# Loading the first three units of an instance norm in shares of partitions

## The chip, the cores and the metric

The kernel runs on one core of one Trainium2 chip. The metric is the device time of one execution in microseconds (us). The times of the kernel before are from three runs; the profile is from one more execution, recorded by the hardware profiler.

## The reference

```python
B, G, C_per_g, H, W = 4, 8, 16, 256, 256
mu = x.mean(axis=(3, 4), keepdims=True)
var = ((x - mu) ** 2).mean(axis=(3, 4), keepdims=True)
out = (x - mu) / np.sqrt(var + 1e-5) * gamma[None, :, :, None, None]
```

Each of the 4 x 8 x 16 = 512 images of 256 x 256 float32 numbers is normalized by its own mean and variance and scaled by the gamma of its channel. The input and the output have 134 MB each, and every number is read once and written once.

## The kernel before

The 512 images are cut into U = 32 units of 16 images. A unit is a tile of 128 partitions with 8192 numbers (32 KB) in each: S = 8 partitions hold one image. In DRAM a unit is one contiguous block of 4 MB, row after row. There are AHEAD = 6 slots in SBUF, named xt0 to xt5; unit u lives in slot u modulo 6, is normalized in place and is stored from there.

Before the loop, `load` (L48) is called for units 0 to 5. Units 1 and 3 are issued on ACT's DMA queue, and units 0, 2, 4 and 5 on SP's. In the profile SP's queue is q1 and ACT's is q10. GpSimd issues two small DMAs of its own: L54 writes a tile of zeros named touch (16 partitions of 128 numbers) into the output, where the first unit's result is written later, and L55 loads gamma. After the loads the program text has 60 no-ops on ACT. Small constants follow, the load of the table for the square root (L78) and a first small root on ACT, and a spread of gamma by 8 matrix products (L88).

The loop over the units does the following for each of them:

- L107: VectorE sums each row of the unit into the first column of st.
- L108: ACT squares the unit and accumulates the squares of each row into the second column. The squares themselves go to a tile named junk.
- L116: TensorE multiplies by a block matrix with -1/65536, which gives every partition the negated mean and mean square of its image.
- L117 to L127: VectorE and ACT make the variance, the root, its reciprocal and the scale, each of one column.
- L130: VectorE adds the negated mean and multiplies by the scale, in place.
- The store of the unit is issued on ACT's queue.
- `load` for unit u + 6 is issued on SP's queue. It goes into the slot that the store is still reading, so SP waits for that store to land.

The order of instructions on each engine is that of the program text. Each DMA on the hardware queues (SP's and ACT's) signals its completion on one of eight semaphores, which are handed out in turn. Where a semaphore is handed out again, the issuing queue first waits for the DMA that had it, unless another wait already implies that.

Of the kernel before, what the change touches and what calls it, by code (L numbers as in the profile page):

```python
# [1 line left out]

# [4 lines left out]

F32 = mybir.dt.float32
U8 = mybir.dt.uint8
ALU = mybir.AluOpType  # L10
ACTF = mybir.ActivationFunctionType
AX = mybir.AxisListType


@with_exitstack
def kernel(
    ctx: ExitStack,
    tc: tile.TileContext,
    x: bass.AP,
    gamma: bass.AP,  # L20
    out: bass.AP,
):
    nc = tc.nc
    B, G, C, H, W = x.shape
    P = nc.NUM_PARTITIONS
    HW = H * W
    n_ch = B * G * C
    S = 8
    K = P // S
    F = HW // S  # L30
    U = n_ch // K
    NG = (G * C) // K
    AHEAD = 6
    assert HW % S == 0 and (G * C) % K == 0

    xv = x.rearrange("b g c h w -> (b g c h w)").rearrange("(u p f) -> u p f", p=P, f=F)
    ov = out.rearrange("b g c h w -> (b g c h w)").rearrange("(u p f) -> u p f", p=P, f=F)
    gv = gamma.rearrange("g c -> (g c)")

    data = ctx.enter_context(tc.tile_pool(name="data", bufs=1))  # L40
    singles = ctx.enter_context(tc.tile_pool(name="singles", bufs=1))
    psum = ctx.enter_context(tc.tile_pool(name="psum", bufs=4, space=bass.MemoryType.PSUM))
    ctx.enter_context(tc.manual_schedule())

    slots = [data.tile([P, F], F32, name=f"xt{i}") for i in range(AHEAD)]

    def load(u, queue):
        queue.dma_start(out=slots[u % AHEAD][:], in_=xv[u])  # L48


    g_row = singles.tile([1, G * C], F32, name="g_row")
    touch = singles.tile([16, 128], F32, name="touch")
    nc.vector.memset(touch[:], 0.0)  # L53
    nc.gpsimd.dma_start(out=ov[0][0::S, 0:128], in_=touch[:])  # L54
    nc.gpsimd.dma_start(out=g_row[:], in_=gv[None, :])  # L55
    for u in range(AHEAD):
        load(u, nc.scalar if u in (1, 3) else nc.sync)

    for _ in range(60):
        nc.scalar.nop()  # L60

    eps_t = singles.tile([P, 1], F32, name="eps_t")
    nc.gpsimd.memset(eps_t[:], 1e-5)
    one = singles.tile([1, 1], F32, name="one")
    nc.gpsimd.memset(one[:], 1.0)
    navg = singles.tile([P, K, S], F32, name="navg")
    nc.gpsimd.memset(navg[:], -1.0 / HW)  # L67
    nc.gpsimd.affine_select(  # L68
        out=navg[:], in_=navg[:], pattern=[[-S, K], [0, S]], compare_op=ALU.is_ge,
        fill=0.0, base=0, channel_multiplier=1,  # L70
    )
    nc.gpsimd.affine_select(  # L72
        out=navg[:], in_=navg[:], pattern=[[S, K], [0, S]], compare_op=ALU.is_ge,
        fill=0.0, base=S - 1, channel_multiplier=-1,
    )
    navg_w = navg[:].rearrange("p k s -> p (k s)")
    root_eps = singles.tile([P, 1], F32, name="root_eps")
    nc.scalar.activation(out=root_eps[:], in_=eps_t[:], func=ACTF.Sqrt)  # L78
    g_rep = singles.tile([1, NG, K, S], F32, name="g_rep")
    g_ps = psum.tile([P, NG], F32, name="g_ps", bufs=1)  # L80
    g_col = singles.tile([P, NG], F32, name="g_col")

    nc.vector.tensor_copy(  # L83
        out=g_rep[:],
        in_=g_row[:].rearrange("o (n k) -> o n k", n=NG).unsqueeze(3).to_broadcast([1, NG, K, S]),
    )
    for n in range(NG):
        nc.tensor.matmul(  # L88
            out=g_ps[:, n : n + 1],
            lhsT=g_rep[:, n].rearrange("o k s -> o (k s)"),  # L90
            rhs=one[:],
            start=True, stop=True,
        )
    nc.vector.tensor_copy(out=g_col[:], in_=g_ps[:])  # L94

    junk = singles.tile([P, F], U8, name="junk")

    st = singles.tile([P, U, 2], F32, name="st")
    nvar = singles.tile([P, U], F32, name="nvar")
    std = singles.tile([P, U], F32, name="std")  # L100
    rstd = singles.tile([P, U], F32, name="rstd")
    scale = singles.tile([P, U], F32, name="scale")

    squares = []
    for u in range(U):
        t = slots[u % AHEAD]
        nc.vector.reduce_sum(out=st[:, u, 0:1], in_=t[:], axis=AX.X)  # L107
        square = nc.scalar.activation(  # L108
            out=junk[:], in_=t[:], func=ACTF.Square, accum_out=st[:, u, 1:2],
        )  # L110
        if u:

            tc.declare_no_dep(square.ins, squares[-1].ins, reason="junk, ordered by the root between")
        squares.append(square)
        ps = psum.tile([P, 2], F32, name="ps")
        nc.tensor.matmul(out=ps[:], lhsT=navg_w, rhs=st[:, u], start=True, stop=True)  # L116
        nc.vector.tensor_scalar(  # L117
            out=nvar[:, u : u + 1], in0=ps[:, 0:1], scalar1=ps[:, 0:1],
            scalar2=ps[:, 1:2], op0=ALU.mult, op1=ALU.add,
        )  # L120
        nc.scalar.activation(  # L121
            out=std[:, u : u + 1], in_=nvar[:, u : u + 1], func=ACTF.Sqrt,
            bias=eps_t[:], scale=-1.0,
        )
        nc.vector.reciprocal(out=rstd[:, u : u + 1], in_=std[:, u : u + 1])  # L125
        g = u % NG
        nc.vector.tensor_mul(  # L127
            out=scale[:, u : u + 1], in0=rstd[:, u : u + 1], in1=g_col[:, g : g + 1],
        )
        nc.vector.tensor_scalar(  # L130
            out=t[:], in0=t[:], scalar1=ps[:, 0:1], scalar2=scale[:, u : u + 1],
            op0=ALU.add, op1=ALU.mult,
        )
        nc.scalar.dma_start(out=ov[u], in_=t[:])
        if u + AHEAD < U:
            load(u + AHEAD, nc.sync)


# [1 line left out]
_INS = ['x', 'gamma']  # L140
_OUTS = [((4, 8, 16, 256, 256), 'float32')]


# [23 lines left out]
```

## Time and profile before

| What | Value |
|---|---|
| Median of three runs | 627.39 us (626.88 to 627.53) |
| Span of the profiled execution | 624.9 us |
| VectorE, ACT, TensorE busy | 443.4, 238.8, 21.4 us |
| HBM read and written | 134.22 and 134.23 MB, 430 GB/s over the span |
| Load on SP's queue, issue to landing | 38.5 us, median of 30 |
| Load on ACT's queue, issue to landing | 31.5 us, median of 2 |
| Store, issue to landing | 62.5 us, median of 32 |
| Waits of SP's queue for stores | 534.4 us in 26 waits |

The profiled execution has no time beside its span, which runs from the first to the last instruction. The median of the runs is 2.5 us longer than that span: it takes in what lies around the instructions. The landing times of loads and stores are longer than the 9.6 us in which 4 MB would move at 436 GB/s, since two queues share the 16 DMA engines and a transfer also waits for those ahead of it in its queue. In a row of the table of windows, the columns are: the window, its length, the busy time of PE, PEld, DVE, ACT and POOL with the number of instructions, the granted clock, the mean share of the DMA engines, and GB/s. In a row of the chain of waits, they are the start, the length and what the time went to.

### The profile page before, as it was taken

To read this page: it belongs to the slowest core of one execution; us is meant where nothing else is said; L and a number is where in the kernel's file an instruction comes from. 1 tells how busy PE (TensorE), PEld (TensorE's weight loads), DVE (VectorE), ACT (ScalarE), POOL (GpSimd) and SP (SyncE) were. 2 spreads that over 40 slices of the span, in tenths; PEclk is the share of its full clock that TensorE was granted. 3 is DMA by queue.
4 is the path that set the end of the run, shared out by engine and by line. 5 is a ranking of instruction groups with operands and counts; after the bars stand their busy time and mean duration, and the time that the engine had idled before them with its cause. 6 is when DMAs were issued, how large, how long until landed. Compare 5 with 4: busy or idle time off the path is not lost.

```text
span 624.9 us, 631 instructions
## 1 busy us (share of the span) xinstructions
PE 21.4 (3%) x80; PEld 19.5 (3%) x80; DVE 443.4 (71%) x163; ACT 238.8 (38%) x98; POOL 2.4 (0%) x11
## 2 busy tenths in 40 slices
PE   0200000000000000000000000000000000000000
PEld 0200000000000000000000000000000000000000
DVE  0588999999776687666786767867668676687730
ACT  0444444444443234432344423444224442244400
POOL 1000000000000000000000000000000000000000
DMA  8999999999999999999999999999999999999998
GB/s 370 436 426 430 422 434 436 436 436 437 432 424 433 436 436 424 436 436 434 436 436 432 422 436 436 434 426 436 436 434 436 436 434 419 436 436 434 426 436 369
DMA packets 9282, 268.46 MB, mean 430 GB/s; under 512 B 1072, under 2 KB 1088, under 8 KB 1088
## 3 DMA queue, kind: packets, MB, share of 16 engines
q10 hardware_dynamic: 4896, 142.61, 52.9%
q1 hardware_dynamic: 4320, 125.83, 46.8%
q0 software_dynamic: 64, 0.01, 0.0%
q14 instruction: 2, 0.02, 0.0%
HBM read 134.22 MB, written 134.23 MB: 430 GB/s over the span
## 4 chain that ended last, share of the span: by engine, by line
another core or an unknown queue 61%; DMA 17%; DVE 15%; SPq 1%; PE 1%; issue 0%; ACT 0%
DVE st L107 10%; DMA xt<-in_x_dram 10%; DMA out_dram<-xt 8%; DVE xt L130 5%; SPq L48 1%; PE ps L116 1%; ACT std L121 0%; DVE nvar L117 0%; DVE rstd L125 0%; DVE scale L127 0%
## 5 line engine op out<-in xcount | busy, mean ns | idle before, releaser
L107 DVE TENSOR_REDUCE st<-xt 128x1 f32<-128x8192 f32 x32 | 277.9, 8685 | 100.4 <-DMA xt<-in_x_dram 100.4
L108 ACT ACTIVATE junk<-xt 128x8192 uint8<-128x8192 f32 x32 | 225.0, 7030 | 275.1 <-DMA xt<-in_x_dram 231.9
L130 DVE TENSOR_SCALAR xt<-xt,ps,scale 128x8192 f32<-128x8192 f32 x32 | 145.6, 4550 | 1.2
L121 ACT ACTIVATE std<-nvar,eps_t 128x1 f32<-128x1 f32 x32 | 9.4, 294 | 79.6 <-DVE nvar L117 79.6
L116 PE MATMUL ps<-st,navg 128*128 128x2 f32 x64 | 17.9, 349 | 557.1 <-DVE st L107 557.1
L116 PEld LDWEIGHTS ps<-st,navg 128*128 128x128 f32 x64 | 16.0, 311 | 558.9 <-issue 558.9
L117 DVE TENSOR_SCALAR nvar<-ps 128x1 f32<-128x1 f32 x32 | 9.2, 287 | 23.8 <-PE ps L116 23.8
L125 DVE RECIPROCAL rstd<-std 128x1 f32<-128x1 f32 x32 | 5.2, 164 | 11.6 <-ACT std L121 11.6
L83 DVE COPY g_rep<-g_row 1x1024 f32<-1x1024 f32 x1 | 0.7, 681 | 14.3 <-DMA g_row<-in_gamma_dram 14.3
L108 ACT ACTIVATION_READ_ACCUMULATOR junk<-xt 128x1 f32 x32 | 6.0, 186 | 0.0
L127 DVE TENSOR_TENSOR scale<-rstd,g_col 128x1 f32<-128x1 f32 x32 | 5.1, 159 | 1.1
L88 PE MATMUL g_ps<-one,g_rep 1*128 1x1 f32 x16 | 3.5, 347 | 16.1 <-DVE g_rep L83 16.1
L88 PEld LDWEIGHTS g_ps<-one,g_rep 1*128 1x128 f32 x16 | 3.5, 325 | 16.1 <-issue 16.1
L94 DVE COPY g_col<-g_ps 128x8 f32<-128x8 f32 x1 | 0.2, 166 | 3.7 <-PE g_ps L88 3.7
L78 ACT ACT_TABLE_LOAD x1 | 1.3, 1283 | 1.7 <-PEq L151 1.7
L53 DVE MEMSET touch<- 16x128 f32 x1 | 0.2, 165 | 0.9 <-PEq L151 0.9
L54 POOL DMA_DIRECT2D out_dram<-touch x1 | 0.6, 619 | 0.8 <-DVE touch L53 0.8
L55 POOL DMA_DIRECT2D g_row<-in_gamma_dram x1 | 0.5, 487 | 0.0
L68 POOL TENSOR_SCALAR_AFFINE_SELECT navg<-navg 128x128 f32<-128x128 f32 x1 | 0.4, 400 | 0.1
L72 POOL TENSOR_SCALAR_AFFINE_SELECT navg<-navg 128x128 f32<-128x128 f32 x1 | 0.4, 399 | 0.1
L67 POOL MEMSET navg<- 128x128 f32 x1 | 0.2, 232 | 0.0
L78 ACT ACTIVATE root_eps<-eps_t 128x1 f32<-128x1 f32 x1 | 0.2, 203 | 0.0
(6 smaller groups left out, 0.6 us busy)
## 6 DMA issues: line engine op xcount, KB each, us to landing
out_dram<-xt ACTq DMA_DIRECT2D x32, 4096.0 KB, 62.5
xt<-in_x_dram SPq DMA_DIRECT2D x30, 4096.0 KB, 38.5
xt<-in_x_dram ACTq DMA_DIRECT2D x2, 4096.0 KB, 31.5
out_dram<-touch POOLq DMA_DIRECT2D x1, 8.0 KB, 9.1
g_row<-in_gamma_dram POOLq DMA_DIRECT2D x1, 0.5 KB, 13.3
```

The source lines that it names most:

```text
L48: queue.dma_start(out=slots[u % AHEAD][:], in_=xv[u])
L78: nc.scalar.activation(out=root_eps[:], in_=eps_t[:], func=ACTF.Sqrt)
L83: nc.vector.tensor_copy(out=g_rep[:], in_=g_row[:].rearrange("o (n k) -> o n k", n=NG).unsqueeze(3).to_broadcast([1, NG, K, S]),)
L88: nc.tensor.matmul(out=g_ps[:, n : n + 1], lhsT=g_rep[:, n].rearrange("o k s -> o (k s)"), rhs=one[:], start=True, stop=True,)
L107: nc.vector.reduce_sum(out=st[:, u, 0:1], in_=t[:], axis=AX.X)
L108: square = nc.scalar.activation(out=junk[:], in_=t[:], func=ACTF.Square, accum_out=st[:, u, 1:2],)
L116: nc.tensor.matmul(out=ps[:], lhsT=navg_w, rhs=st[:, u], start=True, stop=True)
L117: nc.vector.tensor_scalar(out=nvar[:, u : u + 1], in0=ps[:, 0:1], scalar1=ps[:, 0:1], scalar2=ps[:, 1:2], op0=ALU.mult, op1=ALU.add,)
L121: nc.scalar.activation(out=std[:, u : u + 1], in_=nvar[:, u : u + 1], func=ACTF.Sqrt, bias=eps_t[:], scale=-1.0,)
L125: nc.vector.reciprocal(out=rstd[:, u : u + 1], in_=std[:, u : u + 1])
L127: nc.vector.tensor_mul(out=scale[:, u : u + 1], in0=rstd[:, u : u + 1], in1=g_col[:, g : g + 1],)
L130: nc.vector.tensor_scalar(out=t[:], in0=t[:], scalar1=ps[:, 0:1], scalar2=scale[:, u : u + 1], op0=ALU.add, op1=ALU.mult,)
```

## The change

Units 0, 1 and 2 are no longer loaded by one DMA each. A table gives for each of them a list of shares (first partition, step), and `load` issues one DMA for each share, on the same queue as before. For units 0 and 1 these are every 8th partition from 0, every 8th from 4, every 4th from 2 and every 2nd from 1: 16, 16, 32 and 64 partitions. For unit 2 they are every 4th from 0, every 4th from 2 and every 2nd from 1: 32, 32 and 64. All other units are loaded as before. The large and small transfers on the hardware queues are 72 in all, in place of 64. The 60 no-ops are dropped from the text.

```diff
+    shares = {
+        0: ((0, S), (S // 2, S), (S // 4, S // 2), (1, 2)),
+        1: ((0, S), (S // 2, S), (S // 4, S // 2), (1, 2)),
+        2: ((0, S // 2), (S // 4, S // 2), (1, 2)),
+    }
+
     def load(u, queue):
-        queue.dma_start(out=slots[u % AHEAD][:], in_=xv[u])
+        for first, step in shares.get(u, ((0, 1),)):
+            queue.dma_start(out=slots[u % AHEAD][first::step], in_=xv[u][first::step])
...
     for u in range(AHEAD):
         load(u, nc.scalar if u in (1, 3) else nc.sync)
-
-    for _ in range(60):
-        nc.scalar.nop()
```

## The prediction

> **What bounds the kernel now.** I read the page first, for its engines, its slices and its DMA queues; then the chain of work that ended last; then a table of windows over the whole span; and last the packet records of the trace, one record for each row of 32 KB that a DMA engine moves.
>
> ```profile
> span 624.9 us, 631 instructions
> ...
> PE 21.4 (3%) x80; PEld 19.5 (3%) x80; DVE 443.4 (71%) x163; ACT 238.8 (38%) x98; POOL 2.4 (0%) x11
> ...
> DMA  8999999999999999999999999999999999999998
> ...
> q10 hardware_dynamic: 4896, 142.61, 52.9%
> q1 hardware_dynamic: 4320, 125.83, 46.8%
> ...
> L107 DVE TENSOR_REDUCE st<-xt 128x1 f32<-128x8192 f32 x32 | 277.9, 8685 | 100.4 <-DMA xt<-in_x_dram 100.4
> ```
>
> The busiest compute engine is VectorE with 71%, and it idles 100.4 us for loads. The two queues (q10 is ACT's, q1 is SP's) fill 52.9 + 46.8 = 99.7% of the time of 16 DMA engines. So the bound is the DMA engines, in every slice. From the chain of waits:
>
> ```profile
> 0.80 21.80 DMA xt<-in_x_dram
> ...
> 33.10 4.55 DVE xt L130
> ...
> 546.72 38.51 DMA xt<-in_x_dram
> ...
> 595.73 4.55 DVE xt L130
> ```
>
> Units 0 and 1 share the engines and arrive together at 22.6. The first store is issued after 33.10 + 4.55 = 37.65; until then the two rings hold loads only, and the six loads (25.2 MB at 436 GB/s, 58 us) outlast that. The last apply ends at 600.3, while stores run to 623. At 436 GB/s the store of one unit takes 9.6 us, so the last store could be issued some 13 us later without moving the end. Compute therefore has slack at both ends, and the time is: start of the first row + 512 rows for each DMA engine + what follows the last row. The windows show each of these:
>
> ```profile
> 0.00:1.50 1.50, 0.00 (x0) 0.00 (x0) 0.17 (x1) 0.00 (x0) 0.35 (x5) 1.00 0.00 0
> 1.50:2.00 0.50, 0.00 (x0) 0.00 (x0) 0.00 (x0) 0.28 (x1) 0.50 (x2) 1.00 1.98 590
> 2.00:3.00 1.00, 0.00 (x0) 0.00 (x0) 0.00 (x0) 1.00 (x1) 0.93 (x5) 1.00 0.70 229
> ...
> 4.00:22.00 18.00, 3.54 (x16) 3.48 (x16) 0.85 (x2) 0.00 (x0) 0.00 (x0) 1.00 1.00 432
> 22.00:38.00 16.00, 0.56 (x2) 0.50 (x2) 14.20 (x6) 7.42 (x3) 0.00 (x0) 1.00 1.00 434
> 38.00:44.00 6.00, 0.00 (x0) 0.00 (x0) 6.00 (x1) 5.92 (x1) 0.00 (x0) 1.00 0.92 350
> ...
> 100.00:580.00 480.00, 14.51 (x52) 13.03 (x52) 356.12 (x130) 190.63 (x78) 0.00 (x0) 1.00 1.00 433
> ```
>
> The last two numbers are the DMA share and GB/s, counted by the packets that start in the window. In 1.50:2.00, 590 GB/s are nine rows, and a share of 1.98 is 1.98 x 0.5 x 16 / 9 = 1.76 us a row. In 100:580 a row takes 32.8 KB x 16 / 433 = 1.21 us. So the first rows are stretched by about 0.5 us. In 38:44 the same happens a second time: the packet records show 10.3 us of stretch in all, 0.64 an engine, where the first store joins the loads. Nowhere else is there anything to win: between 100 and 580 the rows stand back to back. The sum for one engine: first row from 1.80 to 2.67, ending between 3.48 and 4.06 in the records; 511 more at 1.21 (619); last rows end between 622.7 and 623.6; the span ends at 624.9. The runs' median is 627.39, so 2.5 us lie around the span, and I leave them as they are.
>
> **The change, part by part.** *The no-ops:* ACT's instructions in the profile hold no no-op, and the table load starts at 1.72, right behind the two load issues (0.80 + 0.88). Dropping them removes nothing: 0.
>
> *Eight more transfers.* SP gets five more (three for unit 0, two for unit 2), ACT three. Bytes, rows and the 8 rows that each engine moves of a unit stay the same; only their order changes (rows 0, 4, 2, 6, then the odd ones of each eight). Each transfer adds one semaphore packet per engine: the records give it 9 ns, the next row beginning 6 ns after it. 8 x 6 ns = 0.05 us.
>
> *Issue time.* Two ACT issues took 0.88 us, so 0.44 each. Four shares keep SP and ACT until about 2.6, but the first is issued at 0.80 as before, and each engine then has a row from each ring, until 1.80 + 2 x 1.21 = 4.2 at least; the second shares, issued by 1.7, are there in time. Cost 0. Were a share later than its predecessor's row, an engine would idle for the difference.
>
> *New waits on the issuing queues.* There are eight completion semaphores for the hardware queues, and eight shares now take them all. In the built order ACT's issue of unit 3 waits for unit 1's first share, SP's three shares of unit 2 for unit 0's first, unit 1's second and unit 0's second share, unit 4 for unit 0's third, and unit 5 for unit 1's last. With two rings taking turns, row n of an engine ends at about 2.5 + 1.21 n. Those shares end with rows 1, 2, 3, 4, 7 and 16: at 3.7, 4.9, 6.1, 7.3, 11.0 and 21.9, and the semaphore follows some 0.5 later (unit 0 and 1: row end 22.1, landing 22.6). Needed are units 2 and 3 by 22, unit 4 by 41 (when unit 2 is done) and unit 5 by 61. The margins are 14 us and more. Behind ACT's waiting issue stand its table load (1.28 us) and the small root: they move from 1.7 to about 6 and end near 7.5, and the first square needs them at 22.62. Behind SP's waits stand only its other loads, of which the seventh waits for store 0 anyway. The first square and reduction wait for four semaphores in place of one, some tens of ns on an engine with slack. Cost 0 in all; a margin used up would cost idle DMA time one for one.
>
> *The ramp.* No hardware transfer of 16 rows is in the trace, so its start has to be bounded. If the first rows began and ran no better, the gain is 0. If all began at 1.80 and took 1.21, they would end at 3.01 in place of 3.74 on the engine that ends last (4.06 at worst): at most 0.7 to 1.0 us. In the other direction, each of the three boundaries that both rings now reach together could stretch a row as the first ones are stretched: 3 x 0.6 = 1.8 us more. The nearest rows speak for little: the first rows end together (3.48 to 4.06) however early they began, and the row that began last, at 2.67, took only 1.22. So what they wait for was common to all, and a shorter list of descriptors for each engine need not shorten it. At the boundary between units 0, 1 and units 2, 3 near 22 us, both rings end a transfer, and the windows on its two sides show 432 and 434 GB/s with no gap in the records. I take 0.25 us of gain here, a third of the smaller bound.
>
> [...]
>
> The sum: 0 + 0.05 + 0 + 0 - 0.25 = -0.2 us, so a span of 624.7 and 627.39 - 0.2 = **627.2 us**.
>
> **The rivals.** *Drain at each boundary (slower).* The engine finishes a share, signals, and starts the next only when the writes are confirmed. What a transfer takes beyond its data bounds the price: 21.8 us from issue to landing less 8.39 MB at 436 GB/s (19.2) is 2.6. The three boundaries common to both rings would give 7.8 us, and 635.0; at the 0.6 of a stretched first row, 1.8 us, and 629.2. It decides from 0.5 us a boundary. Against it: in the steady stretch a unit (one load, one store) comes every 19.36 us in the chain, and 8.39 MB at 436 take 19.24, so two transfers cost 0.12 beyond their data; and the boundary at 22 us shows none. What speaks for it is only that shares of one row were never seen. [...]
>
> *Both stretches go (faster).* If the stretches of 0.6 us at the start and at 41 us come from long lists of descriptors put up at once (unit 4's first row is the one stretched at 41), issuing in shares with waits between removes both: 1.0 + 0.64 = 1.6 us, and 625.8. For it: the stretch sits on first rows of a transfer. Against it: unit 5's first row at 61 us is not stretched, and the stretch at 41 falls where the first store starts, which does not change.
>
> *The shares don't spread.* If a share of 16 rows ran on two engines, with eight rows each as in a whole unit, the first engine would get 32 rows each of units 0 and 1 and 24 of unit 2, in place of 8: 64 more, 64 x 1.21 = 77 us, and some 704. Against it: the 16-row store of the touch tile, though on the software queue, shows 16 packets within 0.6 us, each between two rows of a different engine.
>
> **How the numbers follow.** My forecast gets 0.80, the drain 0.07, both stretches gone 0.10, no spreading 0.03. A measurement of this kernel can tell about 0.2%, 1.25 us, from no change; the forecast itself leaves that band on each side with 0.01. So faster 0.11, same 0.78, slower 0.11. The range goes down to the faster rival, 625.8, and up by the spread of the three runs (0.65) and a part of the boundary's price: 628.5.
>
> **What would show it.** Right: q10 with 4944 packets and q1 with 4400 (16 more for each added transfer), the DMA digits unchanged, 432 to 434 GB/s in 4:22, units 0 and 1 still landing together near 22.5, the table load near 6 us, and the stretch in 38:44 still there. Wrong: fewer than 425 GB/s in 4:22 (a drain), a gap near 22, 41 or 61 us (a late issue), a window of 38:44 near 430 (the second stretch gone), or DMA engines that end tens of us apart.

## The result and the profile after

The changed kernel takes 632.08 us (median of four runs, 631.92 to 632.32) against 627.26 for the kernel before on the same chip: a ratio of 1.0079 with a 95% interval of 1.0064 to 1.0093. It is slower by 4.8 us, where 0.2 us of gain were forecast. The profiled execution has a span of 630.1 us, 5.2 more than before.

The page of the kernel after:

```profile
span 630.1 us, 648 instructions
...
DMA  8999999999999999999999999999999999999997
GB/s 234 433 433 433 433 433 433 433 433 431 433 433 433 433 433 435 433 433 433 433 433 433 433 433 435 435 435 437 435 437 435 433 435 433 433 435 437 433 433 339
...
q10 hardware_dynamic: 4944, 142.61, 52.9%
q1 hardware_dynamic: 4400, 125.83, 46.7%
...
L112 DVE TENSOR_REDUCE st<-xt 128x1 f32<-128x8192 f32 x32 | 277.9, 8684 | 107.0 <-DMA xt<-in_x_dram 107.0
```

The DMA digits are nearly those of before: 9 in all slices but the first and the last. What is new is the first number of the second row: 234 GB/s in the first slice, where the kernel before had 370. The row of the kernel before:

```profile
GB/s 370 436 426 430 422 434 436 436 436 437 432 424 433 436 436 424 436 436 434 436 436 432 422 436 436 434 426 436 436 434 436 436 434 419 436 436 434 426 436 369
```

The slices are 15.6 and 15.75 us long, so 5.78 MB came in before and 3.69 MB after. The difference of 2.09 MB is 4.8 us at 433 GB/s, about the whole loss. The windows of the kernel after say the same:

```profile
0.00:1.50 1.50, 0.00 (x0) 0.00 (x0) 0.17 (x1) 0.00 (x0) 0.34 (x5) 1.00 0.00 0
1.50:2.00 0.50, 0.00 (x0) 0.00 (x0) 0.00 (x0) 0.00 (x0) 0.50 (x2) 1.00 0.00 0
2.00:3.00 1.00, 0.00 (x0) 0.00 (x0) 0.00 (x0) 0.00 (x0) 0.93 (x5) 1.00 2.33 524
...
4.00:22.00 18.00, 3.54 (x16) 3.48 (x16) 0.85 (x2) 1.49 (x2) 0.00 (x0) 1.00 0.99 321
22.00:38.00 16.00, 0.11 (x1) 0.14 (x1) 8.69 (x1) 7.12 (x2) 0.00 (x0) 1.00 1.00 430
38.00:44.00 6.00, 0.45 (x2) 0.36 (x2) 5.08 (x5) 0.29 (x1) 0.00 (x0) 1.00 1.00 431
44.00:100.00 56.00, 2.24 (x8) 2.01 (x8) 51.28 (x21) 29.67 (x12) 0.00 (x0) 1.00 1.01 437
100.00:580.00 480.00, 14.11 (x51) 12.73 (x52) 358.33 (x127) 192.54 (x77) 0.00 (x0) 1.00 1.00 433
```

In 4:22 the DMA engines are busy (a share of 0.99) and move 321 GB/s in place of 432. So they don't idle between shares; their rows take longer. The packet records of the trace give the durations of single rows, in the order in which each ring (the rows that one queue has waiting at an engine) moves them (medians over 16 engines):

| Row of the ring | Transfer | Before, us | After, us |
|---|---|---|---|
| SP 1, 2 | unit 0, the two shares of 16 partitions after | 1.75, 1.21 | 2.56, 2.56 |
| ACT 1, 2 | unit 1, the two shares of 16 partitions after | 1.22, 1.21 | 2.36, 2.31 |
| ACT 3 | unit 1, first row of the share of 32 | 1.21 | 1.67 |
| SP 3 to 8, ACT 4 to 8 | the shares of 32 and 64 partitions | 1.21 | 1.21 to 1.22 |

Each engine moves four rows in the shares of 16 partitions, and these take about twice the 1.21 us of the others in the table, ACT 3 apart. The records add up as follows, as means per engine. Stretch is what rows take beyond 1.213 us. In the first 16 us it is 5.35 in place of 0.49, so 4.86 more; the first row starts 0.31 later (2.37 in place of 2.06); and the stretch between 36 and 44 us is gone but for 0.02, so 0.62 less. That is 4.55, and the engines end their last rows 4.61 later on average (627.68 in place of 623.07). The engine that ends last does so 5.08 later (628.68 in place of 623.60); the rest of 0.5 is that the engines end further apart.

The timeline of the kernel after, ACT alone (start, length, engine, line, operation, and in brackets the idle time before it and what ended it):

```profile
6.47 1.28 ACT L83 ACT_TABLE_LOAD   x1 [6.47 <-DMA xt<-in_x_dram]
7.76 0.20 ACT L83 ACTIVATE root_eps<-eps_t 128x1 f32<-128x1 f32 x1
29.04 7.03 ACT L113 ACTIVATE junk<-xt 128x8192 uint8<-128x8192 f32 x1 [21.08 <-DMA xt<-in_x_dram]
...
44.11 0.35 ACTq L139 DMA_DIRECT2D out_dram<-xt  x1
```

The first square starts when unit 0 has landed, at 29.04 in place of 22.62, 6.4 us later. The table load has moved behind the wait of ACT's queue, but is done long before. The first store is issued at 44.11 in place of 37.68. The late arrival costs nothing itself, since loads keep the DMA engines busy; the DMA time lost does.

### The profile page after: what moved, and what is told of

Same layout as the page of the kernel before. It is cut to its first block, busy times and chain, and to the rows that moved or that the text cites. A ratio compares the mean times of both kernels' runs of the same rounds, so it can differ in the third digit from the quotient of the medians.

```text
span 630.1 us, 648 instructions
## 1 busy us (share of the span) xinstructions
PE 21.4 (3%) x80; PEld 19.5 (3%) x80; DVE 443.4 (70%) x163; ACT 238.8 (38%) x98; POOL 2.4 (0%) x11
## 3 DMA queue, kind: packets, MB, share of 16 engines
q10 hardware_dynamic: 4944, 142.61, 52.9%
## 4 chain that ended last, share of the span: by engine, by line
another core or an unknown queue 60%; DMA 19%; DVE 12%; issue 2%; SPq 1%; PE 1%; ACT 0%; ACTq 0%; DVEq 0%
DMA xt<-in_x_dram 12%; DVE st L112 8%; DMA out_dram<-xt 7%; DVE xt L135 4%; SPq L56 1%; PE ps L121 1%; ACT std L126 0%; DVE nvar L122 0%; DVE rstd L130 0%; DVE scale L132 0%; ACTq L56 0%; DVEq L112 0%
```

## The experiments

Four theories stood against each other; the expectations call them theories 1 to 4, in this order. *Crowding*: 16 engines each write one row, and the 16 partitions of such a share get in each other's way when they are written together. (The expectations speak of write paths into SBUF; the runs show no such path, only how long rows take.) *Pitch*: 16 engines read addresses 256 KB apart, which collide in DRAM. *Single rows*: a transfer with one row for each engine is slow, wherever it goes. *Start*: rows are slow because the kernel has just begun. The ratios below are to the kernel before on the same chip (median 627.11 to 627.13).

### Other DRAM addresses, same partitions

```diff
-            queue.dma_start(out=slots[u % AHEAD][first::step], in_=xv[u][first::step])
+            queue.dma_start(out=slots[u % AHEAD][first::step], in_=xv[u][row : row + n])   # row: running sum of n = P // step
```

> The shares keep their partitions in SBUF (every 8th, and so on), but read contiguous rows of the unit from DRAM, so 16 engines no longer read 256 KB apart; the rows of units 0, 1 and 2 land in other partitions than in the reference. After the change, the four one-row shares of units 0 and 1 took 2.3 to 2.6 us a row in place of 1.21, some 5 us in all. Theory 1 (16 partitions at step 8 crowd the SBUF side, two engines on one write path): the same slow rows, 632. Theory 2 (reads 256 KB apart collide in DRAM): rows at 1.21, about 627.5. Theory 3 (a transfer of one row per engine can't overlap its read and its write, whatever its place): slow rows, 632.

Measured: 631.76 us, a ratio of 1.0073 (1.0058 to 1.0088). SP's two rows take 2.56 and 2.56, ACT's 2.05 and 2.35. In 4:22 this kernel moves the same 321 GB/s:

```profile
4.00:22.00 18.00, 3.54 (x16) 3.48 (x16) 0.85 (x2) 1.49 (x2) 0.00 (x0) 1.00 0.99 321
```

The reads are now 32 KB apart, and nothing has changed. The pitch is out.

### Blocks of neighbouring partitions

```diff
-        0: ((0, S), (S // 2, S), (S // 4, S // 2), (1, 2)),
+        0: ((0, 16), (16, 32), (32, 64), (64, 128)),       # low, high; unit 1 the same, unit 2 whole
```

> Units 0 and 1 in shares of neighbouring partitions (0 to 15, 16 to 31, 32 to 63, 64 to 127), unit 2 whole. [...] Theory 2: the reads are 32 KB apart and should be quick, 627. Theory 3: only the four one-row shares are slow, 632, and the rows of the larger shares take 1.21.

Measured: 656.06 us, 1.046 (1.0445 to 1.0476): 28.95 us more, far above the 627 and 632 of theories 2 and 3. Crowding alone gives no figure here; it lets rows be slower where the partitions lie closer. The two shares of 16 neighbours take 4.5 to 4.85 us a row past the very first row, and the shares of 32 and of 64 partitions 2.42 to 2.56 in nearly all rows, though an engine moves two and four rows in each of these. The windows of this kernel over the time in which units 0 and 1 come:

```profile
4.00:10.00 6.00, 0.00 (x0) 0.00 (x0) 0.00 (x0) 0.00 (x0) 0.00 (x0) 1.00 0.95 104
10.00:22.00 12.00, 0.00 (x0) 0.00 (x0) 0.00 (x0) 1.49 (x2) 0.00 (x0) 1.00 0.98 124
22.00:36.00 14.00, 3.32 (x16) 3.35 (x16) 0.68 (x1) 0.00 (x0) 0.00 (x0) 1.00 1.09 225
36.00:50.00 14.00, 0.22 (x2) 0.13 (x1) 0.17 (x1) 0.00 (x0) 0.00 (x0) 1.00 0.92 187
```

Compare 104 and 124 with a quarter of 433 (108), and 225 and 187, whose mean is 206, with half of it (217). The rates lie near a quarter and a half of the full one, and go by where the rows land. A row past the first takes near two times the 1.21 us of a whole unit at step 8 (2.31 to 2.56) and in the blocks of 32 and 64, and near four times in a block of 16. What the rows wait for, no run shows.

### Shares that were quick, for all three units

```diff
-        0: ((0, S), (S // 2, S), (S // 4, S // 2), (1, 2)),
+        0: ((0, S // 2), (S // 4, S // 2), (1, 2)),        # unit 1 the same
```

> Units 0, 1 and 2 all in the shares that only unit 2 had: every 4th partition from 0, every 4th from 2, every 2nd from 1; no transfer of one row per engine. Theories 1 and 3: rows near 1.21 from the first ones, as unit 2's shares had, and 626.5 to 627.5. Theory 2: 128 KB between the engines' rows may still cost something, 627 to 630. If the longer issues of shares (0.6 to 0.8 us in place of 0.4) are what delays the start, the first rows begin at 2.2 as after the change, 0.4 later than before.

Measured: 628.0 us, 1.0014 (1.0004 to 1.0023). In units 0 and 1 the rows past the first one take 1.21 to 1.24, and 4:22 is back at full rate:

```profile
4.00:22.00 18.00, 3.54 (x16) 3.48 (x16) 0.93 (x3) 1.19 (x3) 0.00 (x0) 1.00 1.02 437
```

So the large loss needs the shares of 16 partitions at step 8. But shares are no gain here either, and slower by about 0.9 us. The stretch between 36 and 44 us, 0.64 in the kernel before, is 0.88 here and falls on unit 2's last row too (1.63). The first rows start at 2.14, and the issues of these shares take 0.55 to 0.83 us, where a whole unit's takes 0.33 to 0.46 in most cases. In the blocks of neighbours (385 and 413 ns for the first two issues) the first row started at 1.82. So the longer issue goes with the step over partitions, not with the small size.

### The same shares in the middle of the run

```diff
-        0: ...   1: ...   2: ...
+        20: ((0, S), (S // 2, S), (S // 4, S // 2), (1, 2)),
```

> All early units whole; only unit 20 comes in the four shares, in the middle of the run, where loads and stores alternate. Theories 1, 2 and 3: its two one-row shares take 2.4 us a row, each up to 1.2 more, so up to 2.4 us: 627.3 to 629.7; under theory 1 less where the engines are out of step. If the slow rows belong to the start of the kernel (theory 4), the rows of unit 20 take 1.21, and 627.3.

Measured: 629.25 us, 1.0036 (1.0022 to 1.005). Unit 20's two rows take up to 2.00 and 2.10 us, and the rows of the stores in between 1.30 to 1.47. The records hold 1.6 us of stretch per engine there. The window in which they move, which carried 423 GB/s in the kernel before:

```profile
300.00:351.00 51.00, 1.15 (x4) 1.00 (x4) 26.15 (x11) 12.87 (x7) 0.00 (x0) 1.00 1.00 433
351.00:361.00 10.00, 0.56 (x2) 0.50 (x2) 8.82 (x5) 4.43 (x3) 0.00 (x0) 1.00 1.01 364
361.00:400.00 39.00, 1.11 (x4) 1.00 (x4) 33.02 (x12) 18.38 (x7) 0.00 (x0) 1.00 1.00 433
```

The slow rows don't belong to the start. 2.1 us for one unit at 350 us is the same kind of loss.

### Only unit 0 in shares

```diff
-        1: ...   2: ...
         0: ((0, S), (S // 2, S), (S // 4, S // 2), (1, 2)),
```

> Only unit 0 in its four shares, units 1 and 2 whole. Theory 1: half as many crowded rows as after the change (two per engine in place of four), but they alternate with rows of unit 1, which stay on paths of their own, so engines that drift apart may hide part: 0.4 for the later start plus up to 2 x 1.2, so 627.5 to 630.0. If the cost came with every added transfer or with unit 1's queue, it would not halve.

Measured: 630.56 us, 1.0057 (1.0042 to 1.0072), which is above the expected range. Unit 0's two rows take 2.03 and 2.16 (medians), but the rows of unit 1 behind them are stretched too, to 1.69 and 1.71. It looks as if an engine that is held up in a crowded row passes this on to its next row, but no run tests this. In the first 16 us the stretch is 3.5 us per engine, against 5.35 with both units and 0.49 with none: it grows with the number of crowded rows, though not in proportion. Since the cost fell but did not halve, this run alone does not rule out a cost of each added transfer; the matched pair below does.

### One row for each engine, every 7th partition

```diff
+    sevenths = [slice(f, f + 106, 7) for f in range(7)] + [slice(112, 128)]
+    shares = {0: sevenths, 1: sevenths}
```

> Units 0 and 1 each in eight shares of 16 partitions, so one row per engine in every transfer: seven shares with every 7th partition (from 0 to 6), and the last with partitions 112 to 127; unit 2 whole. [...] Theory 3 (a transfer of one row per engine is slow by itself): all rows of the first seven shares take 2.4 us or more, 14 x 1.2 + 7 = 24 us more, some 651.

Measured: 669.48 and 673.14 us in two runs (the second is the profiled one), and 685.16 and 687.26 in two more: further off than the 651 of theory 3. (Its 7 us agree with two rows of 16 neighbours, 4.5 to 4.85 us each in the blocks of neighbours, beyond 1.21.) By crowding the time depends on which of these partitions get in each other's way, which no run had shown. The rows are mixed. SP's shares from partitions 3 and 4 have medians of 1.27 us (a few rows up to 2.49) and 1.41, but SP's five others take 2.3 to 2.5 on nearly all engines. ACT's seven take 1.86 to 2.25, and those from 3 and 4, with 1.86 and 1.95, are not quick. The stretch of the first 44 us alone is 20.7 us per engine, against 1.1 in the kernel before. Behind it the engines are far out of step, single rows stay stretched through the run, and they end apart:

```profile
GB/s 219 244 250 433 437 429 428 418 422 420 418 420 420 420 422 410 431 412 431 418 416 426 418 426 433 435 422 433 433 420 410 435 418 437 426 431 429 416 299 129
```

This run says only that a share with one row for each engine can move near full rate (1.27), and that its partitions matter. Why the shares from 3 and 4 are quicker on SP's queue, and the others slow on nearly all engines, stays open.

### A matched pair: 16 partitions at step 4, from 32 or from 0

```diff
+    first16 = [slice(32, 96, 4), slice(2, P, 4), slice(1, P, 2), slice(0, P, 4)]   # its twin: slice(0, 64, 4) first
+    shares = {0: first16, 1: first16}
```

The kernel of the diff brings the partitions from 32 to 92 first, its twin those from 0 to 60. Theory 1 takes for granted that the first set does not crowd and the second does; no run before shows it, the rows below do.

> Units 0 and 1 each in four transfers: 16 partitions first (every 4th from 32 to 92), then every 4th from 2, every 2nd from 1 and every 4th from 0, which brings the first 16 partitions' rows once more; so each engine moves one extra row for each of the two units. Unit 2 whole. [...] Theory 1 (crowding): the one-row shares take near 1.21 us, but for the stretch that every first row has; 627.1 + 0.4 for the later start + 2 extra rows of 1.21 = 630. Theory 3 (one row per engine is slow by itself): 2.4 us a row, and 632.4, the same as with the partitions from 0 to 60.

> [...] Theory 1: both one-row shares take 2.4 us, 2.4 us more in all than its twin, some 632.4. Theory 3: no difference between the two.

The two kernels have the same number of transfers, rows, steps and waits, and differ only in the 16 partitions that come first. With the partitions from 32 to 92, SP's one-row share takes 1.21 us (1.21 to 1.22 over all 16 engines), and ACT's, which is the first row of all, 1.79, as first rows do. With those from 0 to 60 they take 2.57 and 2.29. The window of 4 to 10 us, first of the kernel with partitions 32 to 92, then of its twin:

```profile
4.00:10.00 6.00, 0.00 (x0) 0.00 (x0) 0.36 (x1) 1.49 (x2) 0.00 (x0) 1.00 1.00 427
```

```profile
4.00:10.00 6.00, 0.00 (x0) 0.00 (x0) 0.00 (x0) 0.39 (x1) 0.00 (x0) 1.00 0.95 280
```

427 against 280 GB/s: a transfer of one row for each engine is not slow by itself. The rows settle crowding against single rows. The times do not: 632.49 us (630.16 to 633.07) and 632.90 (631.74 to 634.22), with ratios of 1.0077 and 1.0092 whose intervals overlap, where 2.4 us of difference were expected. The twin came as theory 1 said (632.4); of the kernel with 32 to 92 only one run of four did (630.16, where 630 was expected), and three took 632.4 to 633.1. In its profiled run, 0.74 us of stretch per engine returned near 44 us, which its twin doesn't have; 14 of the 16 engines end their last rows between 625.6 and 626.5, but two end at 628.3 and 628.85, and those set the end; the twin's all end between 627.3 and 628.35. So most engines had kept the gain of the quick first rows, and two had lost it later; why these two is open.

### Only unit 2 in shares, and unit 3 on the other queue

```diff
-        0: ...   1: ...
         2: ((0, S // 2), (S // 4, S // 2), (1, 2)),
```

> Only unit 2 in its three shares (every 4th partition from 0, from 2, every 2nd from 1), units 0 and 1 whole. All theories: rows at 1.21, first rows at 1.8 as before, 627.1. If shares cost something by their number alone (more issues, more semaphores), a part of the 0.9 us that shares of every 4th partition cost for all three units shows here too.

Measured: 628.12 us, 1.0016 (1.0006 to 1.0025), 1.0 us more than expected. The first rows start at 1.83 as before and the rows are quick (433 GB/s in 22:36), but the stretch between 36 and 44 us is 1.1 us per engine in place of 0.64, and the last row ends at 624.45 in place of 623.60. So here the cost comes neither from the start nor from crowding, and shares for unit 2 alone cost as much as the quick shares for all three units. Why the stretch grows stays open.

```diff
-        load(u, nc.scalar if u in (1, 3) else nc.sync)
+        load(u, nc.scalar if u == 1 else nc.sync)          # kernel before
```

> The kernel before, with unit 3 loaded on SP's queue in place of ACT's. In the kernel before the rows near 41 us are stretched by 0.64 us an engine, where ACT's ring goes over from the load of unit 3 to the first store; after the change, where the first store came when that ring was empty, they were not. If the handover in one ring is the cause, ACT's ring is empty here at the first store and the stretch goes: 0.6 us less, 626.5. If it comes with the first store in any case: 627.1.

Measured: 627.66 us, 1.0009 (0.9999 to 1.0018): no gain. The stretch between 36 and 44 us is still there, and twice as large (1.28 us). The handover inside one ring is not its cause. What makes it, and why it is missing after the change, stays open; it is 0.6 us.

No version ran faster than the kernel before.

## Why the prediction was wrong

**The step that failed** is the first sentence on the eight transfers: bytes, rows and each engine's rows stay the same, "only their order changes". It left out that it matters which partitions are in flight together. In a whole unit 16 engines write at full rate (1.21 us a row), and with partitions 0, 8, 16 and so on they write at half rate (2.31 to 2.56). Each of four rows per engine took 0.8 to 1.35 us more. That each engine keeps its rows does not fit the runs either. The packet records don't say which partition a row belongs to. But if an engine moved 8 neighbouring partitions of a whole unit in order, the 16 rows in flight would again lie 8 partitions apart, since the engines start SP's second rows within 0.57 us of each other; yet whole units run at 1.21 us a row. So the rows of a whole unit seem to be dealt out in another way than the prediction took for granted; which way, no run shows. The term of the ramp, bounded between 1.0 us of gain and 1.8 us of loss and taken as 0.25 of gain, was really 4.9 of stretch and 0.3 of a later start. Its bounds came from first rows and from boundaries between whole units, neither of which has anything to say on a set of partitions that no transfer in that trace had written together. The 16-row store of the touch tile read 16 neighbouring partitions, with 512 bytes a row, and wrote none.

**The drain** was given 629.2 to 635.0, and the measured time lies in there, by another mechanism: its sign came (321 GB/s in 4:22, where fewer than 425 were to mean a drain), but the engines don't wait at a boundary (DMA share 0.99).

**Not spreading** was priced at 77 us, as one of two opposites: 16 engines or two. The shares did spread over 16 engines. What counts is where their rows land, and that was not among the rivals.

**Issue time.** 0.44 us each was forecast from whole units. A share with a step takes 0.6 to 0.83, and the first row starts at 2.20 in place of 1.80. The cost was taken as 0 and was 0.3 to 0.4.

**The stretch at 38 to 44** was expected to stay and went (431 GB/s in place of 350), a gain of 0.62 that the total hides. The window alone doesn't show this, since the first store is issued only at 44.11 after the change, and its first rows move from 47.5 on; but 44:100 moves 437 GB/s, and its rows hold 0.01 us of stretch per engine.

**What held:** the packets of both queues (4944 and 4400), the no-ops (neither kernel has any among ACT's instructions), the table load near 6 us (6.47), the waits for semaphores with no idle ring behind them, 433 GB/s from 100 us to 580, and compute that has slack at both ends: units 0 and 1 landed 6.4 us late and DMA alone set the end.

## What to carry to other kernels

When a transfer is split by partition, ask which partitions are written at the same moment and not only how many engines move them: 16 partitions at step 8 (2.3 to 2.6 us a row), or 32 in a row (2.4 to 2.6 in most rows), moved at about half rate, 16 in a row (4.5 to 4.85) at about a quarter, and 16 at step 4 from 32 (1.21) at full rate. What decides between these sets, no run shows. This kernel keeps the DMA engines busy from end to end, and 4.9 us of stretch at its start cost it 4.8 us, though the late data itself was hidden. A busy share near 1.0 is no sign of full rate (0.99 beside 321 GB/s here): read the GB/s beside it.

## What the runs showed of the hardware

- A load of 32 KB rows by 16 engines takes 1.21 us a row over all 128 partitions, 2.3 to 2.6 over 16 partitions at step 8 or at step 4 from 0, 2.4 to 2.6 in most rows over blocks of 32 or 64, 4.5 to 4.85 over a block of 16 past the very first row, and 1.21 again over 16 partitions at step 4 from 32.
- Issuing a load with a step over partitions took 0.55 to 0.83 us in the first microseconds, and 0.58 to 0.66 in the middle of the run, against 0.33 for a whole unit there.
- Where half of the rows were crowded, some of the rows between them were stretched too (1.69 and 1.71 us beside 2.0 to 2.2).
